# Moving side work in a two-layer encoder kernel: output-weight sums, token-tile loads, a b21 load and one product of the output pairs

## The chip, the cores and the metric

The kernel runs on one core of one Trainium2 chip. The time is the device time of one execution in microseconds; the figure for a kernel is the median over several executions. The engines are TensorE (PE in the profile, with its weight loads as PEld), VectorE (DVE), ScalarE (ACT), GpSimd (POOL) and SyncE (SP), which issues most of the transfers. Each engine runs its own instructions in order; semaphores order them between engines. The transfers go over 16 DMA engines.

## The reference

The input is 2048 prompt tokens and 512 sample tokens with 1024 channels, each going through two layers and a last norm.

```python
def attention_layer(x, g, w_in, w_out, sink, rel_bias):
    h = rmsnorm(x, g)
    z = h @ w_in                      # q (1024), k (256), v (256), gate (1024)
    o = banded_gqa_with_sink(q, k, v, rel_bias, sink)   # 16 heads, 4 kv heads, |i - j| <= 128
    return x + (o * jax.nn.silu(gate)) @ w_out

def fourier_layer(x, g, w_gate, w_out):
    h = rmsnorm(x, g)
    f = jnp.fft.fftn(h.reshape(b, s, 4, 256), axes=(1, 3), norm="ortho").real.reshape(b, s, d)
    gate = h @ w_gate
    return x + (f * jax.nn.silu(gate)) @ w_out

# trunk: attention_layer, fourier_layer, rmsnorm(x, final_norm)
```

`rmsnorm` divides each token's row by the root of its mean square, so it needs the sum of squares of every row of x.

## The kernel before

All arithmetic is in fp32. A product of two fp32 matrices is made from parts: each operand is split into a high part and the rest, and `matmul3` (L92) issues three matmuls, hi x hi, hi x lo and lo x hi. Splits are made by a cast on ScalarE (the high part) and a subtraction on VectorE or GpSimd (the low part).

**The attention phase** (L134) works through five chunks of 512 tokens: chunk 0 is the sample, chunks 1 to 4 the prompt. For each chunk, `make_h` (L170) loads the transposed tokens (xk), `kv_proj` (L267) makes keys and values, and then a loop of 69 steps i runs over eight head pairs p of eight steps each (four blocks of 128 queries, two heads). In step i stand: the scores of one block and head (TensorE spt, L422), bias and minimum (VectorE S, L434), the exp (ScalarE S, L438), reciprocal and scaling (VectorE, L441 and L444); three steps later the transposes of that block (TensorE pt, L461), which wait for the scaled exps, with their split (ScalarE L462, VectorE L463); two steps after that the product with the values (av, L475) and, every second block, that is every four steps, `out_evac` (L480): VectorE's sums o (L492), GpSimd's o times the gate s (L494), ScalarE's cast uT (L495) and GpSimd's lower part uT (L496). In between are the projections of the next head pair (`qg_proj`), as filling for TensorE, and in the last head pair the output projection `out_proj` (op, L94 to L96).

Into the same loop go side jobs, at steps that are written out by hand:

- `stats(c + 1)` (L143), for the next chunk: for each of its four or five token tiles (the prompt's first three chunks read one tile past their end) one step loads the tile (SP, xs, L151, 512 KB) and squares it with a sum (ScalarE, L152); a last step makes the inverse root (`inv_rms`, VectorE L88 and GpSimd L89). The steps lie at i = 28, 32, 36 and so on. At i = 56 `spread` (L157) transposes the result (TensorE L166) and copies it (ScalarE L167).
- `EXTRA[c]` (L629), for chunks 1 to 4: `gate_sums` (load, lower, sums, more) and `out_sums` (load, two sums, four splits) prepare sums of quarters of the gate weight and of the output weight of the Fourier layer, for products in Strassen's manner (seven products in place of eight). Each makes a quarter of the work per chunk. The loads are w32g (L575) and w32e (L607), the sums run in pieces of 256 columns on GpSimd (L565), the splits cast on ScalarE (L581 wB21, L622 eT1, eT3, eT2, eN4), and GpSimd issues the stores to b21d, sumd and the four ftd arrays.
- `AHEAD` in chunk 4 loads what the Fourier phase reads first.

The tiles xs, w32g, w32e, wB21, the four e tiles and (from chunk 1 on) xk share one ring of four buffers (`xtile`, L80): a load or a cast into the next buffer waits until what was in it four tiles ago is read, or has been stored. In chunk 0 the raw rows of the output weight (w32o, L111) use the same ring. Where an instruction is put into the order by hand, `after` (L129) ties it behind the last exp issued.

**The Fourier phase** (L744) makes the gates of the second layer pair by pair (`Pair`, `gates`, L881): W, Z and X are accumulators, the hooks between the products prepare the next pair. The product X (`x_step`, L888) uses four b21 tiles per pair, which `more()` (L873) loads on SP into a ring of 16 buffers; each `x_step` calls `more()` once after its matmuls, as long as tiles are left, and two are loaded ahead at the start. For the last pair the hooks load the rows of the output weight (w32f, `f_load`), the gathered gates (s2) and the first position transforms, whose results us are transposed by `split_T` (tru, L777).

Behind it come the position transforms and the output product. For the last groups (position pairs k1 = 1, 7, 3, 5 of the prompt) class `Outs` (L1138) makes the output product of two tiles of 128 tokens in Strassen's manner. `operands` (L1178) transposes the two tiles, makes the four sums F and splits them into S[1] to S[4], and splits the tiles' own quarters into A (`own`). `products` (L1191) adds the products into the rows xa and xb: W = A[0,0]*wo[0:4], Z = S1*T1, then T2 (in `third`), S4 with wo[12:16], S3*T3, X = A[0,1]*wo[4:8] and A[1,1]*N4. hooks[2] holds the operands of the next pair (`turns`, with its transposes, and the loads that go with it). X completes xa, which is then normed (`normed`: ScalarE's Square jkf, `inv_rms`, VectorE's scaling L1117, and the store). N4 completes xb. In the last pair xb is squared and written in halves.

Of the kernel before, what the change touches and what calls it, by code (L numbers as in the profile page):

```python
# [8 lines left out]
F32 = mybir.dt.float32  # L9
# [3 lines left out]
AF = mybir.ActivationFunctionType  # L13
# [5 lines left out]
P = 128  # L19
D = 1024  # L20
# [24 lines left out]
def encoder(  # L45
# [34 lines left out]
    def xtile(shape, dtype, name):  # L80
        return xp.tile(shape, dtype, align_bytes=LINE, tag="x", bufs=4, name=name)
# [4 lines left out]
    def inv_rms(ss, n, name):  # L86
        inv = main.tile([P, 8], F32, tag="inv", bufs=2, name=name)
        DVE.tensor_scalar(inv[:, :n], ss[:, :n], 1.0 / D, EPS, ALU.mult, ALU.add)  # L88
        POOL.tensor_tensor(inv[:, :n], inv[:, :n], mhalf[:, :n], ALU.pow)  # L89
        return inv  # L90
# [38 lines left out]
    def after(ins, anchor):  # L129

        if anchor is not None:
            tc.add_manual_dep(ins.ins, anchor.ins.name, ISSUE, reason="issue order")

    def attention_phase():  # L134

        with ExitStack() as es:
# [6 lines left out]
            def stats(c):  # L143

                tok, lo_t, hi_t = CHUNKS[c]
                nt = min(640, hi_t - tok) // P
                ss = main.tile([P, 8], F32, tag="ss", bufs=2, name=f"ss{c}")

                def one(i):
                    xt = xtile([P, D], F32, f"xs{c}_{i}")  # L150
                    after(SP.dma_start(xt, x[tok + i * P : tok + (i + 1) * P, :]), last_exp[0])  # L151
                    sq = ACT.activation(xt, xt, AF.Square, accum_out=ss[:, i : i + 1])  # L152
                    after(sq, last_exp[0])

                return [lambda i=i: one(i) for i in range(nt)] + [lambda: inv_rms(ss, nt, f"inv{c}")]

            def spread(c, inv, place=None):  # L157

# [467 lines left out]
                where = (("T1", 0, 1), ("T3", 1, 1), ("T2", 0, 0), ("N4", 1, 0))  # L626
                return [load, lambda: sums(0), lambda: sums(1)] + [lambda a=a: split(*a) for a in where]

            EXTRA = {c: dict(zip((4, 8, 12, 16, 18, 20, 22, 25, 30, 34, 38), gate_sums(c - 1) + out_sums(c - 1))) for c in range(1, 5)}  # L629

            def quarters(place, k):

# [111 lines left out]
    def fourier_phase(tail):  # L744
        with ExitStack() as es:
# [119 lines left out]
            def prod(out, a, b, ks, first):  # L865

                for k in ks:
                    cs = slice(k * P, (k + 1) * P)
                    matmul3(out, (a[0][:, cs], a[1][:, cs]), b[k], first and k == 0, k == 3, not first)
# [3 lines left out]
            def more():  # L873

                k = len(b21)
                if k < 4 * len(pairs):
                    t = right([P, 2, 512], F32R, f"b21_{k}")
                    SP.dma_start(f32(t), f32(b21d[k % 4]))
                    b21.append((t[:, 0], t[:, 1]))

            def gates(pr, hooks):  # L881

                n, A, S = pr.n, pr.A, pr.S
                W = psum2.tile([P, 512], F32, tag="acc", name=f"W{n}")
                Z = psum2.tile([P, 512], F32, tag="acc", name=f"Z{n}")
                X = bank(f"X{n}")

                def x_step(k):  # L888
                    prod(X, A[0, 1], b21[4 * n : 4 * n + 4], (k,), True)
                    more()  # L890

                def silu(c, i, half):
                    th = main.tile([P, 512], F32, tag="xr", bufs=3, name=f"gt{pr.ts[i]}_{half}")
                    ACT.activation(th, c, AF.Tanh, scale=0.5)
                    DVE.scalar_tensor_tensor(th, th, 1.0, c, ALU.add, ALU.mult)
                    t = pr.ts[i]
                    dst, t0 = (s2d[0], t) if t < SEQ // P else (s2d[1], t - SEQ // P)
                    POOL.dma_start(dst[t0 * P : (t0 + 1) * P, half * 512 : half * 512 + 512], th)

                def hook(i):  # L900
                    for h in hooks.get(i, ()):
                        h()

                four = range(4)
                c = xtile([P, 2, 512], F32, f"c{n}")
                c11, c22 = c[:, 0], c[:, 1]
                prod(W, A[0, 0], wg["B11"], four, True)
                ACT.copy(c11, W)
                hook(0)
                x_step(0)  # L910
                prod(Z, S[1], wg["T1"], four, True)
                ACT.copy(c22, Z)
                hook(1)
                prod(W, S[2], wg["T2"], four, False)
                c12 = fp.tile([P, 512], F32, tag="c12", bufs=1, name=f"c12_{n}")
                ACT.copy(c12, W)
                hook(2)
                x_step(1)
                prod(Z, S[4], wg["B22"], four, False)
                DVE.tensor_tensor(c12, c12, Z, ALU.add)  # L920
                silu(c12, 0, 1)
                hook(3)
                x_step(2)
                prod(W, S[3], wg["T3"], four, False)
                DVE.tensor_tensor(c22, c22, W, ALU.add)
                silu(c22, 1, 1)
                hook(4)
                x_step(3)
                DVE.tensor_tensor(c11, c11, X, ALU.add)
                silu(c11, 0, 0)  # L930
                hook(5)
                prod(W, A[1, 1], wg["N4"], four, False)
                silu(W, 1, 0)
                hook(6)
# [81 lines left out]
            pr = pairs[0]  # L1016
# [97 lines left out]
            def normed(x2, r):  # L1114

                inv = sumsq(x2, f"f{r[0]}")
                DVE.scalar_tensor_tensor(x2, x2, inv[:, 0:1], gfb, ALU.mult, ALU.mult)  # L1117
                SP.dma_start(out_rows(r), x2)
# [19 lines left out]
            class Outs:  # L1138
# [39 lines left out]
                def operands(self):  # L1178
                    self.turn(0, 0)
                    self.own(0, 0)  # L1180
                    self.turn(1, 0)
                    self.turn(1, 1)
                    self.sums(1)
                    self.sums(2)
                    self.turn(0, 1)
                    self.sums(4)
                    self.sums(3)
                    self.own(0, 1)
                    self.own(1, 1)

                def products(self, hooks, last=False):  # L1191
                    A, S, four = self.A, self.S, range(4)
                    (xa, xb), q = self.x2, (slice(0, 512), slice(512, 1024))
                    W = psum2.tile([P, 512], F32, tag="acc", name=f"Wo{self.n}")
                    Z = psum2.tile([P, 512], F32, tag="acc", name=f"Zo{self.n}")

                    def add(t, half, ps):
                        DVE.tensor_tensor(t[:, q[half]], t[:, q[half]], ps, ALU.add)

                    prod(W, A[0, 0], wo[0:4], four, True)  # L1200
                    add(xa, 0, W)
                    hooks[0]()
                    prod(Z, S[1], ft["T1"], four, True)
                    add(xb, 1, Z)

                    def third():
                        prod(W, S[2], ft["T2"], four, False)
                        add(xa, 1, W)

                    hooks[1](third)  # L1210
                    prod(Z, S[4], wo[12:16], four, False)
                    add(xa, 1, Z)
                    prod(W, S[3], ft["T3"], four, False)
                    add(xb, 1, W)
                    hooks[2]()
                    X = bank(f"Xo{self.n}")
                    prod(X, A[0, 1], wo[4:8], four, True)
                    add(xa, 0, X)
                    normed(xa, self.us[0][1])
                    if last:  # L1220
                        ss = main.tile([P, 8], F32, tag="ss", bufs=2, name="ssl")
                        junk = fp.tile([P, 512], F32, tag="c12", bufs=1, name="jkl").bitcast(BF16)
                        ACT.activation(junk[:, :512], xb[:, q[1]], AF.Square, accum_out=ss[:, 1:2])
                    prod(W, A[1, 1], ft["N4"], four, False)
                    add(xb, 0, W)
                    if not last:
                        normed(xb, self.us[1][1])
                        return
                    ACT.activation(junk[:, :512], xb[:, q[0]], AF.Square, accum_out=ss[:, 0:1])
                    DVE.tensor_tensor(ss[:, 0:1], ss[:, 0:1], ss[:, 1:2], ALU.add)  # L1230
                    inv = inv_rms(ss, 1, "invl")
                    for half in range(2):
                        hs = q[half]
                        DVE.scalar_tensor_tensor(xb[:, hs], xb[:, hs], inv[:, 0:1], gfb[:, hs], ALU.mult, ALU.mult)
                        (SP, ACT)[half].dma_start(out_rows(self.us[1][1])[:, hs], xb[:, hs])
# [292 lines left out]
```

## Time and profile before

| | |
|---|---|
| median of 3 runs | 1666.85 us (1666.19 to 1668.32) |
| the profiled execution: its own time | 1663.9 us |
| its span, first to last instruction | 1662.1 us |
| granted TensorE clock, mean | 0.996 |
| TensorE busy | 1630.8 us, 98% of the span |
| VectorE busy | 1200.5 us, 72% |
| ScalarE busy | 892.8 us, 54% |
| GpSimd busy | 444.9 us, 27% |
| moved by DMA | 367.75 MB, mean 221 GB/s |

A row of the profile gives the engine, the line of the code, the operation, the tile that is written and the tiles that are read. In brackets stands how long the engine was idle ahead of it and what ended that. Rows of waits have the total in us, how many times, and the longest. Attention takes the span up to about 1100 us, the Fourier phase the rest.

### The profile page before, as it was taken

To read this page: it belongs to the slowest core of one execution; us is meant where nothing else is said; L and a number is where in the kernel's file an instruction comes from. 1 tells how busy PE (TensorE), PEld (TensorE's weight loads), DVE (VectorE), ACT (ScalarE), POOL (GpSimd) and SP (SyncE) were. 2 spreads that over 40 slices of the span, in tenths; PEclk is the share of its full clock that TensorE was granted. 3 is DMA by queue.
4 is the path that set the end of the run, shared out by engine and by line. 5 is a ranking of instruction groups with operands and counts; after the bars stand their busy time and mean duration, and the time that the engine had idled before them with its cause. 6 is when DMAs were issued, how large, how long until landed. Compare 5 with 4: busy or idle time off the path is not lost.

```text
span 1662.1 us, 25836 instructions
## 1 busy us (share of the span) xinstructions
PE 1630.8 (98%) x8939; PEld 1401.0 (84%) x8939; DVE 1200.5 (72%) x2851; ACT 892.8 (54%) x2035; POOL 444.9 (27%) x623
## 2 busy tenths in 40 slices
PE   9999999999999999999999999999999999999997
PEld 7888788888898888988888888888888887888885
DVE  6787666878548786478783588858667667888685
ACT  6788634666236664256661466646555455343342
POOL 2456642322404222223214232221112121101010
PEclk9999999999999999999999999999999999999998
DMA  7486886564865555754548745656566468455952
GB/s 300 155 301 242 295 324 223 186 234 141 292 228 187 196 190 195 268 218 171 222 144 318 253 173 197 222 187 254 188 216 234 171 218 333 169 190 196 357 181 79
DMA packets 98909, 367.75 MB, mean 221 GB/s; under 512 B 11947, under 2 KB 22187, under 8 KB 81372
## 3 DMA queue, kind: packets, MB, share of 16 engines
q1 hardware_dynamic: 75948, 276.93, 47.7%
q0 software_dynamic: 21360, 88.13, 13.5%
q8 instruction: 71, 1.16, 0.3%
q10 hardware_dynamic: 1472, 1.05, 0.2%
q14 instruction: 58, 0.48, 0.1%
HBM read 279.01 MB, written 87.06 MB: 220 GB/s over the span
## 4 chain that ended last, share of the span: by engine, by line
PE 70%; DVE 9%; ACT 7%; DMA 6%; issue 5%; POOL 2%; SPq 0%; POOLq 0%; DVEq 0%; ACTq 0%
PE av L475 5%; PE spt L422 5%; PE pt L461 4%; PE op L94 4%; PE op L96 4%; PE op L95 4%; PE qp L94 3%; PE gp L94 3%; PE gp L96 3%; PE qp L96 3%; PE gp L95 3%; PE qp L95 3%; DMA xs<-in_x_dram 2%; ACT S L438 2%; PE W L95 2%
## 5 line engine op out<-in xcount | busy, mean ns | idle before, releaser
L438 ACT ACTIVATE S<-S 128x385 f32<-128x385 f32 (+1 forms) x320 | 191.0, 597 | 66.0 <-DVE S L434 64.3
L463 DVE TENSOR_TENSOR pts<-pt,pts 128x384 fp32r<-128x384 f32 (+1 forms) x320 | 168.3, 527 | 43.4 <-ACT pts L462 40.9
L462 ACT CAST pts<-pt 128x384 fp32r<-128x384 f32 (+1 forms) x320 | 143.4, 452 | 87.4 <-PE pt L461 83.4
L434 DVE CUSTOM_DVE_ANT_0 S<-spt,b 128x385 f32<-128x385 f32 (+1 forms) x320 | 168.5, 527 | 30.0 <-PE spt L422 27.1
L422 PE MATMUL spt<-kwin,qab 128*128 128x384 f32 (+1 forms) x640 | 157.7, 328 | 1.0 <-DVE S L434 1.0
L461 PE MATMUL pt<-ident,S 128*128 128x128 f32 x896 | 150.7, 273 | 6.2 <-ACT S L438 3.4
L494 POOL TENSOR_TENSOR o<-o,s 128x256 f32<-128x256 f32 x75 | 55.4, 738 | 341.3 <-DVE o L492 335.8
L422 PEld LDWEIGHTS spt<-kwin,qab 128*128 128x128 f32 x640 | 117.8, 188 | 28.2 <-DVE S L434 3.6
L475 PEld LDWEIGHTS av<-pts,v 128*128 128x128 f32 x896 | 126.3, 189 | 15.9 <-DVE pts L463 3.3
L475 PE MATMUL av<-pts,v 128*128 128x256 f32 x896 | 137.3, 286 | 2.1 <-DVE qab L371 1.1
L94 PE MATMUL gp<-h,wg 128*128 128x512 f32 x320 | 137.8, 431 | 0.0
L94 PE MATMUL qp<-h,wq 128*128 128x512 f32 x320 | 137.0, 428 | 0.3 <-DVE v L336 0.3
L461 PEld LDWEIGHTS pt<-ident,S 128*128 128x128 f32 x896 | 113.4, 140 | 21.7 <-ACT S L438 4.0
L94 PE MATMUL op<-wo,uT 128*128 128x512 f32 x320 | 126.5, 397 | 1.6 <-ACT invb L167 0.8
L96 PE MATMUL qp<-h,wq 128*128 128x512 f32 x320 | 126.0, 394 | 0.0
L96 PE MATMUL gp<-h,wg 128*128 128x512 f32 x320 | 125.9, 393 | 0.0
L95 PE MATMUL qp<-h,wq 128*128 128x512 f32 x320 | 125.8, 393 | 0.0
L95 PE MATMUL op<-wo,uT 128*128 128x512 f32 x320 | 125.8, 393 | 0.0
L95 PE MATMUL gp<-h,wg 128*128 128x512 f32 x320 | 125.8, 393 | 0.0
L96 PE MATMUL op<-wo,uT 128*128 128x512 f32 x320 | 124.8, 391 | 0.0
L444 DVE TENSOR_SCALAR S<-S 128x384 f32<-128x384 f32 (+1 forms) x256 | 115.9, 453 | 8.0
L441 DVE RECIPROCAL S<-S 128x1 f32<-128x1 f32 x320 | 51.3, 161 | 73.9 <-ACT S L438 70.7
(415 smaller groups left out, 4266.2 us busy)
## 6 DMA issues: line engine op xcount, KB each, us to landing
wo<-wsd SPq DMA_DIRECT2D x32, 1024.0 KB, 5.1
wq<-wsd SPq DMA_DIRECT2D x31, 1024.0 KB, 4.8
wg<-wsd SPq DMA_DIRECT2D x31, 1024.0 KB, 5.9
x<-x1d SPq DMA_DIRECT2D x40, 512.0 KB, 3.8
b<-b21d SPq DMA_DIRECT2D x40, 512.0 KB, 5.6
b<-rowd SPq DMA_DIRECT2D x40, 384.0 KB, 4.5
xs<-in_x_dram SPq DMA_DIRECT2D x23, 512.0 KB, 6.1
s2d<-gt POOLq DMA_DIRECT2D x40, 256.0 KB, 3.7
```

Source lines behind the costliest of these rows:

```text
L94: PE.matmul(out, a[0], b[0], start=start, stop=False, skip_group_check=more)
L95: PE.matmul(out, a[0], b[1], start=False, stop=False, skip_group_check=more)
L96: PE.matmul(out, a[1], b[0], start=False, stop=stop, skip_group_check=more)
L422: PE.matmul(ps[:, 2 + k0 * P : 2 + k1 * P], q, kwin[g][:, part, b * P + k0 * P : b * P + k1 * P], start=part == 0, stop=part == 1,)
L434: DVE.tensor_tensor_reduce(out=s[:, e0:e1], in0=ps[:, 1 + e0 : 1 + e1], in1=st["bias"][:, j, 386 - e1 : 386 - e0][:, ::-1], scale=1.0, sca ...
L438: last_exp[0] = ACT.activation(s[:, e0:e1], s[:, e0:e1], AF.Exp, bias=mn, scale=-1.0, accum_out=den)
L444: DVE.tensor_scalar(s[:, ks], s[:, ks], den, None, ALU.mult)
L461: PE.transpose(ps[:, kb, :], s[:, 1 + kb * P : 1 + (kb + 1) * P], ident)
L462: ACT.copy(hi[:, k0:k1, j, :], ps[:, k0:k1, :])
L463: DVE.tensor_tensor(lo[:, k0:k1, j, :], ps[:, k0:k1, :], f32(hi[:, k0:k1, j, :]), ALU.subtract)
L475: PE.matmul(out, v, pt[:, kb].rearrange("p h q -> p (h q)"), start=kb == k0 and part == 0, stop=kb == k1 - 1 and part == 1,)
L494: eng.tensor_tensor(o, o, s, ALU.mult)
```

## The change

Four edits, none of which changes what is computed:

1. In `stats`, the step that loads tile i no longer squares it; it squares tile i - 1. There is one step more, so each Square and the inverse root come one step of this list, four steps of the loop, later.
2. The steps of `EXTRA` move from 4, 8, 12, 16 (gate weight) and 18, 20, 22, 25, 30, 34, 38 (output weight) to 2, 4, 6, 8 and 10, 12, 14, 16, 18, 20, 22.
3. In the last pair of gates, `more()` is called once more after the first step of X, so that the last b21 tile's load is issued there and not a step later.
4. In `Outs`, the product X with its sum, and xa's norm, are moved: X goes ahead of hooks[2], the norm behind hooks[2], and T3 with its sum behind both. In `operands`, the split of A[0,1] goes ahead of the third sum.

```diff
@@ -146,13 +146,18 @@
                 nt = min(640, hi_t - tok) // P
                 ss = main.tile([P, 8], F32, tag="ss", bufs=2, name=f"ss{c}")
 
+                xs = []
+
                 def one(i):
-                    xt = xtile([P, D], F32, f"xs{c}_{i}")
-                    after(SP.dma_start(xt, x[tok + i * P : tok + (i + 1) * P, :]), last_exp[0])
-                    sq = ACT.activation(xt, xt, AF.Square, accum_out=ss[:, i : i + 1])
-                    after(sq, last_exp[0])
-
-                return [lambda i=i: one(i) for i in range(nt)] + [lambda: inv_rms(ss, nt, f"inv{c}")]
+
+                    if i:
+                        sq = ACT.activation(xs[i - 1], xs[i - 1], AF.Square, accum_out=ss[:, i - 1 : i])
+                        after(sq, last_exp[0])
+                    if i < nt:
+                        xs.append(xtile([P, D], F32, f"xs{c}_{i}"))
+                        after(SP.dma_start(xs[i], x[tok + i * P : tok + (i + 1) * P, :]), last_exp[0])
+
+                return [lambda i=i: one(i) for i in range(nt + 1)] + [lambda: inv_rms(ss, nt, f"inv{c}")]
 
             def spread(c, inv, place=None):
 
@@ -626,7 +631,7 @@
                 where = (("T1", 0, 1), ("T3", 1, 1), ("T2", 0, 0), ("N4", 1, 0))
                 return [load, lambda: sums(0), lambda: sums(1)] + [lambda a=a: split(*a) for a in where]
 
-            EXTRA = {c: dict(zip((4, 8, 12, 16, 18, 20, 22, 25, 30, 34, 38), gate_sums(c - 1) + out_sums(c - 1))) for c in range(1, 5)}
+            EXTRA = {c: dict(zip((2, 4, 6, 8, 10, 12, 14, 16, 18, 20, 22), gate_sums(c - 1) + out_sums(c - 1))) for c in range(1, 5)}
 
             def quarters(place, k):
 
@@ -908,6 +913,9 @@
                 ACT.copy(c11, W)
                 hook(0)
                 x_step(0)
+                if pr is pairs[-1]:
+
+                    more()
                 prod(Z, S[1], wg["T1"], four, True)
                 ACT.copy(c22, Z)
                 hook(1)
@@ -1184,8 +1192,8 @@
                     self.sums(2)
                     self.turn(0, 1)
                     self.sums(4)
+                    self.own(0, 1)
                     self.sums(3)
-                    self.own(0, 1)
                     self.own(1, 1)
 
                 def products(self, hooks, last=False):
@@ -1210,13 +1218,13 @@
                     hooks[1](third)
                     prod(Z, S[4], wo[12:16], four, False)
                     add(xa, 1, Z)
-                    prod(W, S[3], ft["T3"], four, False)
-                    add(xb, 1, W)
-                    hooks[2]()
                     X = bank(f"Xo{self.n}")
                     prod(X, A[0, 1], wo[4:8], four, True)
                     add(xa, 0, X)
+                    hooks[2]()
                     normed(xa, self.us[0][1])
+                    prod(W, S[3], ft["T3"], four, False)
+                    add(xb, 1, W)
                     if last:
                         ss = main.tile([P, 8], F32, tag="ss", bufs=2, name="ssl")
                         junk = fp.tile([P, 512], F32, tag="c12", bufs=1, name="jkl").bitcast(BF16)
```

In the instructions of the changed program each load of a token tile is at least four steps ahead of its Square. On SP the w32e loads stand right behind the weights wg of head pair 3 and ahead of wq of head pair 4, where they stood behind these; the last b21 load stands six loads further ahead. On GpSimd the sequence in a chunk is: sums of w32g, wB21's lower part, the store to b21d, the stores to sumd, the first o and uT of the chunk, the eight pieces of the w32e sums, the next o and uT; before, three pairs of o and uT stood ahead of the w32e sums.

## The prediction

> **What bounds the kernel now.** The first thing read is the head of the page.
>
> ```profile
> span 1662.1 us, 25836 instructions
> PE 1630.8 (98%) x8939; PEld 1401.0 (84%) x8939; DVE 1200.5 (72%) x2851; ACT 892.8 (54%) x2035; POOL 444.9 (27%) x623
> ```
>
> TensorE is busy for 1630.8 of 1662.1 us. No product is added or taken away by this change, so at most the 31.3 us that TensorE stands still can be won, and everything below is about which of those it removes and which it makes. The view of waits by engine, restricted to TensorE, tells what they are; it names only those that the semaphores show.
>
> ```profile
> engine line waited for: us in total, times, longest us
> PE pt L461 <- ACT S L438: 3.4, 2, 2.2
> PE pt L461 <- DVE S L444: 2.5, 2, 1.3
> PE X L94 <- DMA b<-b21d: 2.0, 1, 2.0
> ...
> PE Ap L95 <- DVE gp L1070: 0.7, 3, 0.3
> ```
>
> The largest two are transposes of the attention (pt) that wait for a softmax: ScalarE's exp was late. Next comes one product X that waits for a load of b21. So the question is what makes ScalarE late. The waits of all engines have the line:
>
> ```profile
> ACT xs L152 <- DMA xs<-in_x_dram: 22.8, 9, 4.7
> ```
>
> Nine times ScalarE stood at the Square of a token tile until that tile's load had landed, up to 4.7 us. ScalarE runs in order, so the exps behind stood too. Whether TensorE paid for it shows in its busy time around these Squares (20 us windows: TensorE, its weight loads, VectorE, ScalarE, GpSimd; then the granted clock, the DMA share, GB/s):
>
> ```profile
> 140.00:160.00 20.00, 18.77 (x107) 15.95 (x107) 14.79 (x52) 17.88 (x42) 11.97 (x17) 1.00 0.74 282
> 160.00:180.00 20.00, 17.88 (x103) 14.71 (x102) 16.08 (x58) 16.61 (x44) 16.03 (x24) 1.00 0.95 358
> 340.00:360.00 20.00, 19.60 (x111) 16.36 (x109) 14.97 (x44) 13.49 (x35) 6.86 (x10) 1.00 0.62 211
> 360.00:380.00 20.00, 18.74 (x106) 15.88 (x107) 15.73 (x52) 13.63 (x35) 4.19 (x6) 1.00 0.76 270
> 560.00:580.00 20.00, 18.79 (x108) 16.10 (x107) 14.01 (x42) 12.39 (x30) 5.16 (x8) 1.00 0.70 229
> 580.00:600.00 20.00, 17.63 (x100) 14.74 (x99) 14.56 (x45) 12.33 (x33) 4.94 (x7) 1.00 0.69 249
> 800.00:820.00 20.00, 19.89 (x112) 16.61 (x110) 15.29 (x47) 13.36 (x34) 6.56 (x10) 1.00 0.60 223
> 820.00:840.00 20.00, 18.92 (x110) 16.55 (x111) 17.88 (x55) 13.43 (x36) 3.57 (x5) 1.00 0.43 160
> 1040.00:1060.00 20.00, 20.00 (x118) 17.57 (x117) 16.72 (x56) 13.46 (x36) 4.57 (x7) 1.00 0.53 184
> ```
>
> TensorE stood still for 1.66 us in chunk 1 (40 less 19.60 and 18.74), 3.58 in chunk 2 and 1.19 in chunk 3: together 6.43 us. In the last chunk, which has no token tiles to square, the same place is full (20.00 of 20). In chunk 0 3.35 us are lost, but there ScalarE itself is at 17.88 of 20, so not all of that is a wait.
>
> **Token loads a step ahead.** One of the Squares, the 10 us around it, the landing of all 23 tile loads, and a product o of GpSimd (one comes every four steps):
>
> ```profile
> 795.69 1.06 ACT L152 ACTIVATE xs<-xs 128x1024 f32<-128x1024 f32 x1 [2.92 <-DMA xs<-in_x_dram]
> 790.00:800.00 10.00, 10.00 (x61) 8.76 (x60) 6.37 (x21) 6.72 (x18) 2.62 (x4) 1.00 0.82 296
> DMA to landing us min/median/max: 3.2/6.1/10.1
> 518.00 0.74 POOL L494 TENSOR_TENSOR o<-o,s 128x256 f32<-128x256 f32 x1 [7.46 <-DVE o L492]
> 527.01 0.74 POOL L494 TENSOR_TENSOR o<-o,s 128x256 f32<-128x256 f32 x1 [7.01 <-DVE o L492]
> ```
>
> The tile loads land after 6.1 us, 10.1 at most. Load and Square are issued in the same step now. In the changed program a load stands four steps ahead of its Square, which is 9.0 us (518.00 to 527.01). It can also start earlier, since the output weight's sums, which use the same four buffers, end at step 22 and not at 38. So nearly every load has the time that it needs, and the waits end: **-6.4 us** in chunks 1 to 3, and nothing if the loads still come late (0 to -6.4). The 2.92 us wait at 795.69 is worth a look: TensorE was full around it (10.00 of 10). So ScalarE can be up to 2.9 us late before TensorE stops; as the exps are not everywhere as far ahead, I use 2.4 as this slack below.
>
> In chunk 0 the Squares move four steps later, into the stretch at 17.88 of 20, and the loads of the output weight wait for the buffers that they free. A Square of 1.06 us arriving in a full stretch costs up to +1.2 with its read of the sum; against it stands up to 2.4 us of waiting at Squares that goes (22.8 us in all, of which chunk 0 has little). I take about a third of the 3.35 us, **-1.2**, range -2.4 to +1.2.
>
> **The sums move up.** They are the same instructions on GpSimd, two to sixteen steps earlier. What moves is what stands behind them: GpSimd's product o and its split uT of the attention output, on which ScalarE's cast waits. Chunk 1 and chunk 2 of before (the o at 518.00 is above):
>
> ```profile
> 275.71 1.64 POOL L565 TENSOR_TENSOR w32g<-w32g,w32g 128x256 f32<-128x256 f32 x2 [29.73 <-DMA w32g<-in_w_gate_dram]
> ...
> 296.36 0.74 POOL L494 TENSOR_TENSOR o<-o,s 128x256 f32<-128x256 f32 x1 [7.00 <-DVE o L492]
> 495.89 1.43 POOL L565 TENSOR_TENSOR w32g<-w32g,w32g 128x256 f32<-128x256 f32 x2 [40.67 <-DMA w32g<-in_w_gate_dram]
> ...
> 532.07 1.44 POOL L565 TENSOR_TENSOR w32e<-w32e,w32e 128x256 f32<-128x256 f32 x2 [3.07 <-DMA w32e<-in_w_fout_dram]
> DMA to landing us min/median/max: 3.0/5.3/13.5
> DMA to landing us min/median/max: 6.3/7.0/7.4
> ```
>
> The last two lines are the landings of b21d's transfers and of the w32e loads. In the changed order the eight w32e pieces stand on GpSimd ahead of the o that was at 518.00; before, they came at 532.07, after it. Their second load takes a buffer that comes free only when b21d's store has landed. So in chunk 2: start 495.89, eight pieces of 0.72 and one store of about 0.6 make 6.4, landing of the store 5.3, of the load 7.0, then eight pieces 5.9 (532.07 to 537.9, where o followed): 520.5, and o is 2.5 us late. Chunk 1 by the same sum from 275.71: 300.3 against 296.36, 3.9 late. Chunks 3 and 4 have the same distances as chunk 2 to within half a microsecond; I take 2.5 for each. Less the slack of 2.4: 1.5 in chunk 1 and 0.1 in each other one, **+1.8**. The range is 0 (landings of 3.0 and 6.3 take 3.0 off, and only chunk 1 would be late, by less than the slack) to +5.8 (each a microsecond later). Before, the o's own operands came last ([7.46 <-DVE o]), so these sums would be the new thing that ScalarE waits for, through "uT <- POOL o". The splits behind (T1 to N4) are one cast of 0.6 us each on ScalarE, two steps apart (4.5 us); the windows above have ScalarE under 70% busy in chunks 1 to 3, and I cost them nothing. If a buffer's store is late there, the cast waits and it costs what the Squares cost now.
>
> **The last b21 load.** The chain ahead of the product X:
>
> ```profile
> 1373.24 0.56 SPq L878 DMA_DIRECT2D b<-b21d  x1
> 1384.61 2.35 DVE L1107 TENSOR_TENSOR us<-us,s2s 128x1024 f32<-128x1024 f32 x2
> 1386.78 0.50 PE L94 MATMUL X<-b,tTb 128*128 128x512 f32 x1 [2.00 <-DMA b<-b21d]
> 1387.58 1.69 PE L777 MATMUL tru<-ident,us 128*128 128x128 f32 x14
> 1403.91 0.80 PE L94 MATMUL fo<-wo,tTu 128*128 128x512 f32 x1 [1.25 <-ACT wo L1285]
> ```
>
> The extra call puts this load ahead of six others on SP's queue; six issues of 0.56 put it at about 1369.9. Even with the longest landing of b21d's loads above, 13.5 us, it is there at 1383.4, before TensorE comes to X at 1384.78 (1386.78 less 2.00). X takes 0.8 and ends at 1385.6, but the transposes behind it need us, whose two products end at 1385.8 and 1386.96: 0.2 to 1.4 of the 2.0 us, I take 0.7, stay as a wait for VectorE. **-1.3**, range -2.0 to 0. The six loads that it passes come some 1.3 us later; the next stall, at 1403.91, is ScalarE's split of wo, which hangs on casts that follow TensorE's own pace, so I let it shift along unchanged.
>
> ```profile
> 1400.00:1405.00 5.00, 3.56 (x17) 2.29 (x16) 4.73 (x11) 4.16 (x12) 0.00 (x0) 0.85 1.03 418
> 1405.00:1410.00 5.00, 5.00 (x27) 4.35 (x26) 4.62 (x8) 3.86 (x8) 0.54 (x1) 0.81 1.03 415
> ```
>
> Around this next stall the granted clock falls to 0.85 and 0.81; without it 0.15 and 0.19 of 5 us, 1.7 us, would come back. I leave it in place and let -1.7 widen the low end. [...]
>
> **The product X of the Outs pairs.** It is now issued ahead of the next pair's turns and of T3, in three pairs and in the end. In the inner pairs its split of A[0,1] moves ahead of the third sum; the price is bounded by the largest wait of this stretch on each side, 0.7 us of TensorE in all (Ap above) and this one:
>
> ```profile
> 1574.57 1.23 DVE L1107 TENSOR_TENSOR up<-up,s2p 128x1024 f32<-128x1024 f32 x1 [2.22 <-DMA s2p<-s2d,mir]
> ```
>
> There the gather of s2p waits for a buffer until xb's output is written; xb's end moves back by VectorE's row-norm work, some 0.8 us, xa's forward. TensorE was not waiting there, so I take **+0.3**, range -0.5 to +2.2.
>
> **The tail.** Behind the last product:
>
> ```profile
> 1647.95 0.69 DVE L1198 TENSOR_TENSOR x<-x,Xo 128x512 f32<-128x512 f32 x1 [2.03 <-PE Xo L96]
> 1650.24 0.39 PE L96 MATMUL Wo<-fN,tT 128*128 128x512 f32 x1
> 1650.79 1.28 DVE L1117 SCALAR_TENSOR_TENSOR x<-x,invf,gfb 128x1024 f32<-128x1024 f32 x1 [0.73 <-POOL invf L89]
> 1651.99 0.68 DVE L1198 TENSOR_TENSOR x<-x,Wo 128x512 f32<-128x512 f32 x1
> ```
>
> TensorE's last sum is there at about 1650.65 (1650.24 and 0.39), but VectorE is at the other row's norm (1650.79, 1.28 us) and adds it at 1651.99. With X one product of twelve matmuls earlier (2.72 us) that norm runs from 1648.07 to 1649.35, T3's add from there to 1650.04, and the last add starts at 1650.65: 1.3 earlier, and all behind it moves along. **-1.3**, range -1.4 to -0.7 (if the add of T3 comes in between later).
>
> **Sum**: -6.4 -1.2 +1.8 -1.3 +0.3 -1.3 = -8.1 us. The profiled run took 1663.9 us (1.8 around its span of 1662.1); it becomes 1655.8. It lies 2.95 below the median of the runs shown, 1666.85, so the forecast for the median is **1658.7 us**.
>
> **Rivals.**
> - The loads are still late. The first token tiles take the buffers of the sums' splits, which come free when their stores have landed; if these are slow, the step ahead is lost and the waits of 6.4 us and chunk 0's 1.2 stay, while b21 and the tail give 2.6 and GpSimd takes 1.8: 1666.85 -2.6 +0.3 +1.8 = 1666.4, no change. Against it: the sums end six steps before the first tile load.
> - The reordered Outs pairs cost: X waits for its split, or the gather's 2.22 us reaches TensorE in each of the three pairs, +6.7 in place of +0.3: 1658.7 +6.4 = 1665.1, within the noise. Against it: TensorE's waits there are 0.3 us now.
> - Slower: the sums hold GpSimd. One mechanism, in all four chunks: with L the landing of the second w32e load, TensorE loses 1.8 + 4 x (L - 7.0). All other terms make -9.9, so it is level at L = 9.0 and slower by 0.2% from L = 9.9; at the 10.1 that a tile load has shown it costs 14.2 and the time is 1666.85 -9.9 +14.2 = 1671. For it: the chunk's DMA share is 0.6 to 0.8 and the load now runs beside the sums' three stores. Against it: the eight w32e loads lie between 6.3 and 7.4. [...]
> - More: chunk 0 gives 2.4, GpSimd costs nothing, the clock's 1.7 comes back and the rest as forecast: -6.4 -2.4 -2.0 -0.5 -1.4 -1.7 = -14.4, 1652.5.
>
> **Chances.** Forecast 0.68, loads still late 0.12, Outs pairs 0.05, slower 0.12, more 0.03. A change of under 0.2%, 3.3 us, can't be told from none here. Faster by more than that: 0.68 and 0.03, with a little of the forecast falling short, 0.71; same 0.17; slower 0.12. The range: from the best case, 1652.5, up to 1667, which takes in the two cases without change and leaves out the slower one.
>
> **What would show it.** Right: no Square at L152 waits for its load in chunks 1 to 3, and TensorE is at 20.00 in 340 to 380, 560 to 600 and 800 to 840 or where these steps then lie; X <- b21d is gone from TensorE's waits; the last add on VectorE starts with TensorE's last sum. The w32e pieces would show "<- DMA w32e" right after the sumd stores, and ScalarE's uT <- POOL o a wait of 2 to 5 us once a chunk. Wrong: these waits above 5 us in every chunk with TensorE's idle time beside them (slower), Squares that still wait (no change), or a new wait of the product Xo or of the gather in the pairs 7, 3 and 5.

## The result and the profile after

| | before | changed |
|---|---|---|
| median | 1666.78 us (1665.89 to 1670.75, 6 runs) | 1661.26 us (1660.06 to 1662.93, 6 runs) |
| profiled execution, its span | 1663.9, 1662.1 us | 1662.93, 1661.1 us |

The ratio is 0.9963 with a 95% interval of 0.995 to 0.9976; by the medians the change is 5.5 us faster. A second set of executions of the same changed kernel beside its own runs of before (1662.68 us in 11 runs, 1665.11 in 15) gave 0.9983 (0.9974 to 0.9992), 2.4 us by the medians. Forecast were 8.1 us. The two profiled executions lie only 1.0 us apart, since that of before lies 2.9 us below its median and that of the change 1.7 above its own; so the traces are compared stretch by stretch.

The rows of TensorE's waits in the changed kernel, which stand against those of before:

```profile
PE pt L466 <- DVE S L449: 4.1, 4, 2.1
PE Wo L94 <- DVE x L1206: 2.2, 1, 2.2
PE op L94 <- ACT invb L172: 1.6, 1, 1.6
PE pt L466 <- ACT S L452: 1.4, 2, 0.7
PE fo L94 <- ACT wo L1293: 1.3, 1, 1.3
...
PE tru L782 <- DVE us L1115: 0.7, 2, 0.5
```

X no longer waits for b21; tru waits for us in its place. The transposes pt still wait for a softmax, only elsewhere, op waits 1.6 us for invb, the copied inverse root (0.8 before), and there is a new wait that the prediction did not have: Wo, which is N4, for VectorE's x, 2.2 us. The view of all waits names the softmax's new reason; first a row of before, then rows of the changed kernel:

```profile
ACT uT L495 <- POOL o L494: 63.6, 58, 2.1
```

```profile
ACT uT L500 <- POOL o L499: 100.5, 67, 5.2
...
POOL w32e L570 <- DMA w32e<-in_w_fout_dram: 21.9, 4, 5.9
...
POOL eT L570 <- ACT eT L627: 19.7, 12, 3.3
```

ScalarE's longest wait at uT rose from 2.1 to 5.2 us, GpSimd waits 21.9 us for the w32e loads (11.0 before), and the Squares' line is nearly empty. In the tile view of xs, the 22.8 us have become this:

```profile
  DMA xs<-in_x_dram: 0.3, 1
```

The windows where the Squares had stopped TensorE (the changed kernel, columns as before):

```profile
340.00:360.00 20.00, 20.00 (x118) 17.53 (x117) 16.56 (x53) 14.95 (x40) 3.46 (x5) 1.00 0.48 178
360.00:380.00 20.00, 20.00 (x117) 17.49 (x116) 16.99 (x58) 14.34 (x37) 2.94 (x4) 1.00 0.65 228
560.00:580.00 20.00, 20.00 (x116) 17.45 (x115) 17.03 (x52) 13.93 (x35) 3.33 (x5) 1.00 0.50 178
580.00:600.00 20.00, 20.00 (x119) 17.60 (x118) 17.35 (x55) 14.81 (x37) 3.55 (x6) 1.00 0.61 225
800.00:820.00 20.00, 20.00 (x118) 17.55 (x117) 17.45 (x55) 15.17 (x39) 3.98 (x5) 1.00 0.58 203
820.00:840.00 20.00, 20.00 (x117) 17.50 (x116) 17.55 (x52) 13.43 (x34) 2.94 (x4) 1.00 0.45 151
```

They are full: this part of the change did what it should. What was given back stands in two places. The first is the eight pieces, the sums of w32e in steps of 256 columns on GpSimd. In chunk 1, GpSimd's timeline of the changed kernel:

```profile
281.55 0.57 POOL L588 DMA_DIRECT2D b21d<-wB  x1
...
295.91 1.55 POOL L570 TENSOR_TENSOR w32e<-w32e,w32e 128x256 f32<-128x256 f32 x2 [5.53 <-DMA w32e<-in_w_fout_dram]
297.42 1.43 POOL L570 TENSOR_TENSOR w32e<-w32e 128x256 f32<-128x256 f32 x2
298.81 2.81 POOL L570 TENSOR_TENSOR w32e<-w32e,w32e 128x256 f32<-128x256 f32 x4
301.58 0.73 POOL L499 TENSOR_TENSOR o<-o,s 128x256 f32<-128x256 f32 x1
```

o was at 296.36 before and is at 301.58, behind the pieces. ScalarE stands for it, then TensorE, in the timelines of these engines:

```profile
302.34 0.40 ACT L500 CAST uT<-o 128x256 fp32r<-128x256 f32 x1 [4.99 <-POOL o L499]
```

```profile
304.16 0.52 PE L466 MATMUL pt<-ident,S 128*128 128x128 f32 x3 [2.13 <-DVE S L449]
```

The windows around it show a second price, the granted clock (third column from the end) in the 5 us behind the wait:

```profile
300.00:305.00 5.00, 2.87 (x18) 2.35 (x17) 1.54 (x6) 2.35 (x7) 3.03 (x5) 1.00 0.00 0
305.00:310.00 5.00, 5.00 (x22) 4.46 (x21) 4.70 (x17) 3.64 (x9) 2.24 (x4) 0.66 0.64 190
310.00:315.00 5.00, 5.00 (x30) 4.35 (x29) 3.49 (x13) 3.45 (x10) 3.29 (x5) 1.00 0.50 209
```

At 0.66, 22 matmuls are issued in these 5 us; in the same window of last_pair_old, behind a wait of 2.11, they are 32 at 1.00 (its rows stand in the last section). By an estimate from this row, 0.66 of 5 us being 3.3, 1.7 us are lost at the lower clock besides the 2.13 of the wait. The other place is the tail; first the last product's start in TensorE's timeline, then VectorE:

```profile
1643.80 0.39 PE L96 MATMUL Wo<-fT,S 128*128 128x512 f32 x1
1646.37 0.47 PE L94 MATMUL Wo<-fN,tT 128*128 128x512 f32 x1 [2.18 <-DVE x L1206]
```

```profile
1644.34 1.28 DVE L1125 SCALAR_TENSOR_TENSOR x<-x,invf,gfb 128x1024 f32<-128x1024 f32 x1 [0.73 <-POOL invf L89]
1645.55 0.68 DVE L1206 TENSOR_TENSOR x<-x,Wo 128x512 f32<-128x512 f32 x1
1650.98 0.69 DVE L1206 TENSOR_TENSOR x<-x,Wo 128x512 f32<-128x512 f32 x1 [4.75 <-PE Wo L96]
```

N4 adds into the accumulator W that T3 has just filled, so it may not begin until VectorE has read T3's sum out of it. VectorE reads it at 1645.55, behind xa's scaling. The clock fell here too, in the 5 us in which the wait ends:

```profile
1645.00:1650.00 5.00, 3.63 (x9) 2.87 (x10) 1.23 (x2) 0.72 (x2) 0.00 (x0) 0.67 0.26 105
```

Both kernels issue the same 8939 matmuls. The time from the start of one matmul to the start of another with the same number in a kernel's sequence can thus be subtracted between traces, clock and waits included. A table of such differences to the profiled run of before, in us (plus is slower), with kernels of the experiments that are told below:

| stretch (its place in before) | changed | changed again | loads and sums | b21 alone | loads ahead alone | sums behind o |
|---|---|---|---|---|---|---|
| chunk 0 loop, 86 to 211 | +0.6 | +0.6 | +0.7 | +0.9 | +0.7 | +0.7 |
| chunk 1, pieces of w32e, 280 to 332 | +3.9 | +3.8 | +4.1 | 0 | 0 | 0 |
| chunk 1, Squares, 332 to 413 | -2.9 | -2.9 | -2.9 | +0.3 | -2.9 | -2.9 |
| chunk 2, pieces, 495 to 538 | +0.6 | +0.8 | +0.8 | 0 | 0 | 0 |
| chunk 2, Squares, 538 to 630 | -4.6 | -4.6 | -4.6 | -1.4 | -4.6 | -4.6 |
| chunk 3, pieces | +0.4 | +0.6 | +0.2 | 0 | 0 | 0 |
| chunk 3, Squares | -1.9 | -1.9 | -1.9 | +0.1 | -1.6 | -2.0 |
| chunk 4, pieces | +1.8 | +1.9 | +2.0 | 0 | 0 | 0 |
| last gates, b21, 1377 to 1440 | -1.0 | -1.4 | -0.1 | -2.0 | -0.7 | -1.9 |
| inner Outs pairs, 1561 to 1616 | +0.2 | -0.7 | +0.6 | -0.4 | +0.2 | +0.1 |
| last pair to the last matmul | +4.2 | +4.1 | 0 | 0 | 0 | +2.6 |

"b21 alone" leaves the attention as it was, so its column shows by how much a stretch differs between two executions of the same code: up to 1.4 us at the Squares and 0.9 in chunk 0, but 0 at the pieces.

### The profile page after: what moved, and what is told of

Read it like the earlier page. It is cut to its first block, busy times and chain, and to the rows that moved or that the text cites. A ratio compares the mean times of both kernels' runs of the same rounds, so it can differ in the third digit from the quotient of the medians.

```text
span 1661.1 us, 25834 instructions
## 1 busy us (share of the span) xinstructions
PE 1632.6 (98%) x8939; PEld 1404.2 (85%) x8939; DVE 1201.1 (72%) x2851; ACT 890.5 (54%) x2035; POOL 441.7 (27%) x623
## 3 DMA queue, kind: packets, MB, share of 16 engines
q10 hardware_dynamic: 1472, 1.05, 0.2%
```

## The experiments

Each ran beside its own executions of the kernel before on one chip; the ratio is to those.

**sums_behind_o.** The pieces are tied behind GpSimd's uT, and the last six steps of the output weight's sums move to 13 to 24.

```diff
-zip((2, 4, 6, 8, 10, 12, 14, 16, 18, 20, 22), ...)
+zip((2, 4, 6, 8, 10, 13, 15, 18, 20, 22, 24), ...)
...
+                    else:
+                        last_lo[0] = lo
...
-                        pieces(b22, b22, b12, ALU.subtract)
+                        pieces(b22, b22, b12, ALU.subtract, last_lo[0])
...
```

> The changed kernel, with GpSimd's eight pieces of the output weight's sums tied behind uT of the block before (and the steps 13 to 24 in place of 12 to 22). Theory: in the changed kernel the pieces hold GpSimd's o until the w32e load has landed, which stops TensorE 2.30, 0.61, 0.43 and 1.43 us in chunks 1 to 4 and lowers its clock in chunk 1; behind o they stop nobody: 4.8 to 6.3 us below the changed kernel's 1661.3, so 1655 to 1656.5, no ScalarE wait of over 2 us at uT, and the Squares still wait for no load. Rival: the wait goes elsewhere (to the next o, to the splits' buffers, or back to the token tiles, which now get their buffers later): 1659 to 1662.

Measured: 1655.28 us against 1665.25, ratio 0.9941 (0.9925 to 0.9957). GpSimd's timeline in chunk 1 has o ahead of the pieces, and the window in which the changed kernel stood still is full:

```profile
297.84 0.73 POOL L499 TENSOR_TENSOR o<-o,s 128x256 f32<-128x256 f32 x1 [7.83 <-DVE o L497]
299.09 0.74 POOL L501 TENSOR_TENSOR uT<-o,uT 128x256 fp32r<-128x256 f32 x1 [0.52 <-ACT uT L500]
299.78 1.55 POOL L572 TENSOR_TENSOR w32e<-w32e,w32e 128x256 f32<-128x256 f32 x2
```

```profile
300.00:305.00 5.00, 5.00 (x33) 4.43 (x32) 4.90 (x14) 2.71 (x8) 5.00 (x7) 1.00 0.15 47
305.00:310.00 5.00, 5.00 (x31) 4.41 (x30) 4.02 (x14) 3.39 (x9) 2.80 (x5) 1.00 0.68 242
```

The clock stays at 1.00 too. All four stretches of the pieces fall to 0 in the table, and the Squares keep their gain: the pieces ahead of o were the cause, and in this trace the wait went nowhere else. In the two later kernels that hold this edit, both_mended and both_mended_t3, the pieces' stretch of chunk 1 kept 0.4 and 0.9 us.

**last_pair_old.** T3, X, N4 in the last pair as before; the inner pairs as changed.

```diff
+                    if last:
+                        lower()      # T3 and its sum
+                        cross()      # X and its sum
+                        normed(xa, self.us[0][1])
+                    else:
+                        cross()
+                        hooks[2]()
+                        normed(xa, self.us[0][1])
+                        lower()
```

> The changed kernel, with the last pair's products alone in the order of before (T3, X, N4). Theory: in the changed order N4 adds into the accumulator that T3 has just filled, so TensorE waits 2.2 us until VectorE, which does xa's norm first, has read T3's sum, and restarts at a lower clock (0.67 over 5 us, another 1.7); against it stands the 1.3 us that the last add gains. So 0.9 to 2.5 us faster than the changed kernel: 1658.8 to 1660.4. Rival: the prediction's own step, a gain of 1.3 from the new order: 1662.6.

Measured: 1658.77 us, ratio 0.9961 (0.9945 to 0.9976); from the same stretch of matmuls the last pair takes 0.2 us more than before, not 4.2, and the wait of Wo is gone from TensorE's. By the traces the direction is the theory's: the changed order costs the tail more than it brings. The times alone don't tell it, since the ratio's interval overlaps that of the change.

**last_pair_old_late_norm.** In addition xa's scaling is tied behind the last add:

```diff
-                        normed(xa, self.us[0][1])
+                        write = normed(xa, self.us[0][1], True)
...
-                    add(xb, 0, W)
+                    done = add(xb, 0, W)
+                    if last:
+                        write(done)
```

> As last_pair_old, and xa's scaling by its norm on VectorE is tied behind the last add of N4. Theory: TensorE doesn't wait, and the last add no longer waits 1.3 us for that scaling; the scaling now lies beside ScalarE's last Square and delays what follows by 0.4: 0.9 us faster than last_pair_old, so 1658 to 1659.5. Rival: the end is set by the stores, not by the last add: as last_pair_old.

Measured: 1659.79 us, 0.9969 (0.9957 to 0.9981), above the expected range by 0.3 us and not faster than last_pair_old in the times. In VectorE's timeline the last add does follow N4 at once, and the scaling comes behind it:

```profile
1647.62 0.69 DVE L1210 TENSOR_TENSOR x<-x,Wo 128x512 f32<-128x512 f32 x1 [0.61 <-PE Wo L96]
1648.22 1.28 DVE L1127 SCALAR_TENSOR_TENSOR x<-x,invf,gfb 128x1024 f32<-128x1024 f32 x1
```

From the last matmul's start to the last store's issue it is 4.74 us, in last_pair_old and before 5.79: the 1.05 are there, but smaller than what other places of the program spread by from one execution to the next: the pieces' stretch of chunk 1 alone took 4.3 us more than before in this trace and 2.5 in that of last_pair_old.

**outs_alone.** The kernel before with the Outs edits only (the diff's hunks at L1184 and L1210).

> The kernel before, with the edits in Outs alone (product X, xa's norm, T3, the split of A[0,1]). Theory: the tail loses 0.9 to 2.5 us as told for last_pair_old and the three inner pairs 0.5: 1668.2 to 1669.8 against 1666.8. Rival (the prediction): +0.3 in the pairs and -1.3 in the tail: 1665.8.

Measured: 1667.96 us against 1665.25, ratio 1.0014 (1.0002 to 1.0025). This edit alone makes the kernel slower, by 2.3 us after the ratio (0.3 to 4.2), just below the expected range. The last pair took 2.6 us more here, without a fall of the clock (1.00 from 1640 to 1655), and the end behind the last matmul 1.3 less.

**loads_and_sums.** The kernel before with the token loads and the steps of the sums (the hunks at L146 and L626).

> The kernel before, with the token loads a step ahead and the earlier steps of the sums, nothing else. Theory: the tile waits give 5.8 to 6.4 us, GpSimd's pieces take 4.8 and the clock in chunk 1 up to 1.5 more, chunk 0 takes 0.9: -0.1 to 0 by the profile that I have, but that profile was one of the slower executions; with the medians' 5.5 us less b21's 1.3 and plus the tail's 0.9 to 2.5 it is 1661 to 1664. Rival: nearly all of the measured gain is b21's and Outs': 1666.

Measured: 1661.9 us against 1666.39, 0.9975 (0.9964 to 0.9986). Within the theory's range, so the attention edits carry most of the gain. Its windows show the same fall of the clock as the changed kernel:

```profile
300.00:305.00 5.00, 2.65 (x17) 2.18 (x16) 1.49 (x7) 2.30 (x7) 3.39 (x5) 1.00 0.00 0
305.00:310.00 5.00, 5.00 (x22) 4.38 (x21) 4.73 (x16) 3.70 (x10) 2.02 (x3) 0.66 0.61 142
```

**b21_alone.** The kernel before with the extra `more()`.

> The kernel before, with the extra call of more() alone. Theory: TensorE's 2.0 us wait for b21 goes and 0.7 to 1.0 of it comes back as a wait for us: -1.0 to -1.3, 1665.5 to 1665.8. Rival: the loads that it passes come late and the next stall, fo at wo, grows: 1666.8 or more.

Measured: 1663.7 us against 1666.39, ratio 0.9992 (0.9982 to 1.0003): the median lies below the expected range, but by the ratio there is no difference that these runs can tell from none. TensorE's waits show the exchange that was forecast:

```profile
PE fo L94 <- ACT wo L1288: 1.3, 1, 1.3
...
PE tru L777 <- DVE us L1110: 1.0, 3, 0.5
```

The 2.0 us of X are gone, 1.0 is back at us, and the next stall, the product fo at ScalarE's split wo, stands at 1.3 as before, so the loads that were passed cost nothing there.

**chunk0_old_squares.** The changed kernel, with load and Square in one step for the tiles that are squared in chunk 0.

```diff
+                def one(i, lag=0 if c == 1 else 1):
...
+                    if i < nt and not lag:
+                        square(i)
```

> The changed kernel, but in chunk 0 (the squares of chunk 1's tiles) load and Square stay in one step. Theory: TensorE loses 12.4 us to its ideal pace in 120 to 180 in the changed kernel and 11.6 in the one before, so the later Squares cost up to 0.9 there: 1660.4 to 1661.3. Rival (the prediction): the later Squares gain 1.2: 1662.5.

Measured: 1661.99 us against 1666.39, 0.9982 (0.9973 to 0.9992), between the two ratios of the changed kernel and 0.7 us above the expected range. The chunk 0 stretch took 0.0 us more than before here, 0.6 in the changed kernel, but b21_alone and outs_alone, which have the same old Squares there, took 0.9 and 2.5 more. So the cost that the theory gave to the later Squares can't be told from the spread of single executions. The gain of 1.2 us that was forecast shows in no trace.

**both_mended.** sums_behind_o and last_pair_old_late_norm together.

> The changed kernel with sums_behind_o and last_pair_old_late_norm together. Theory: the two places are independent, so the gains add: 4.8 to 6.3 and 1.8 to 3.4 below 1661.3, 1651.6 to 1654.7. Rival: one of the places only moves its wait: 1655 to 1660.

Measured: 1653.68 us against 1666.39, ratio 0.993 (0.9917 to 0.9944), 7.6 us below the changed kernel's 1661.26 and within the expected range, as it should be if the gains of the two places add. The times don't show the second gain by itself: the interval overlaps that of sums_behind_o alone.

**changed_again.** The changed kernel once more, unedited.

> The changed kernel itself, beside the next three on one chip. Theory: the waits stand where they stood (N4 at T3's add 2.2 us, pt behind the w32e pieces in chunk 1 about 2.1), while the clock's fall behind them comes in some executions and not in others, so that single times spread by 2 to 3 us: median 1660 to 1662. Rival: the places themselves change from run to run.

Measured: 1662.68 us against 1665.11, 0.9983 (0.9974 to 0.9992), slightly above the range. The waits stand at the same places with the same length (Wo 2.2, pt up to 2.1), and the clock fell in chunk 1 again (0.70).

**t3_add_first.** xa's scaling in the last pair tied behind T3's add.

```diff
-                    normed(xa, self.us[0][1])
+                    write = normed(xa, self.us[0][1], last)
                     prod(W, S[3], ft["T3"], four, False)
-                    add(xb, 1, W)
+                    done = add(xb, 1, W)
+                    if last:
+                        write(done)
```

> The changed kernel, with xa's scaling in the last pair tied behind T3's add on VectorE. Theory: N4 waits for nothing but T3's add, which now starts with T3's sum: the wait falls from 2.2 to about 0.9 us (0.7 for the add, the rest for the semaphores), the scaling still ends ahead of N4's sum, and the last add starts with that sum: 1.3 us, or up to 3 with the clock, below the changed kernel. Rival: N4 waits for something else (the transposed tile, the weight): 2.2 us stay.

Measured: 1658.96 us, 0.9961 (0.9947 to 0.9975), against 1662.68 of changed_again beside it. TensorE's timeline:

```profile
1645.08 0.47 PE L94 MATMUL Wo<-fN,tT 128*128 128x512 f32 x1 [0.87 <-DVE x L1210]
```

The wait is 0.87 in place of 2.18 us, the stretch costs 1.3 in place of 4.1. So it is T3's add, held up by the scaling, that N4 waited for. With the 1.3 us that are gained behind the last matmul, this order is about level with that of before, and no better.

**loads_ahead_alone.** The kernel before with the hunk in `stats` alone.

> The kernel before, with load and Square a step apart and nothing else; the sums keep their late steps. Theory: one step of 9 us is enough for most loads, so that most of the 9.4 us (by stretches of equal instructions) go without the earlier sums, and the w32e pieces hold nobody: 1657.5 to 1660. Rival: the sums' splits hold the four buffers until step 38, the loads are issued no earlier and the waits at the Squares stay: 1664 to 1667.

Measured: 1655.53 us against 1665.11, ratio 0.9944 (0.993 to 0.9957); 2 us faster than the expected range's low end. Its windows:

```profile
300.00:320.00 20.00, 20.00 (x117) 17.51 (x116) 16.16 (x51) 12.62 (x32) 8.80 (x12) 1.00 0.52 178
360.00:380.00 20.00, 20.00 (x118) 17.53 (x117) 16.91 (x56) 15.27 (x41) 3.36 (x5) 1.00 0.74 260
580.00:600.00 20.00, 20.00 (x117) 17.50 (x116) 17.30 (x55) 15.04 (x38) 2.94 (x4) 1.00 0.71 254
```

One of the four edits gives all that the change gains and more: 9.6 us by the medians against 2.4 of the whole change beside it. All Squares together wait 0.3 us for their loads here, as in the changed kernel. So the buffers, which the sums still held until step 38, made no Square wait, and the earlier sums weren't needed for it.

**both_mended_t3.** sums_behind_o and t3_add_first together.

> The changed kernel with sums_behind_o and t3_add_first together. Theory: -6.7 us of the pt waits and -1.3 to -3 of the tail: 1652 to 1654.5, as both_mended or 0.3 better, since the end behind the last product is 1.3 shorter than in the kernel before and only 0.9 of wait is paid for it. Rival: the tail's wait brings the lower clock with it again and both_mended is 1 to 2 us faster.

Measured: 1654.21 us against 1665.11, 0.9933 (0.9919 to 0.9946), the same as both_mended by the intervals. Either is faster than both the kernel before and the changed one; loads_ahead_alone overlaps with them.

## Why the prediction was right, and where not

Faster was right, and 1661.26 lies in the range; of the 8.1 us forecast, 5.5 came, and 2.4 in the second set. That the total came out this near is in part luck: terms were off by several us in both directions, and the errors partly cancelled.

- **Token loads a step ahead** (-6.4): the mechanism held, the term was mis-sized. By equal matmuls the three stretches give -2.9, -4.6 and -1.9, together -9.4 us in the same trace, and the medians of loads_ahead_alone give 9.6. Against the two other traces that have the old Squares, b21_alone and outs_alone, it is 8.5 and 9.8. The step that failed is reading TensorE's standstill from busy time in windows: a matmul's busy time overlaps with its neighbour's, as in TensorE's timeline of before, with 0.40 us each at starts 0.23 apart,

```profile
174.93 0.40 PE L95 MATMUL op<-wo,uT 128*128 128x512 f32 x1
175.16 0.40 PE L96 MATMUL op<-wo,uT 128*128 128x512 f32 x1
```

  so a row at 17.63 of 20 has lost more than 2.37: it holds 100 matmuls, the full window of the changed kernel 119.
- **Chunk 0** (-1.2): nothing of it is seen (+0.6 in the table, within the spread). What TensorE gained there (av and spt wait 0.9 us less) it lost at other waits. In 86 to 212 it waits 1.4 us for pt <- ACT S and 1.6 for op <- ACT invb in the changed kernel, 0.3 and 0.8 in before; loads_ahead_alone has 1.4 and 1.7, and chunk0_old_squares 0.3 and 0.8 again. Before and changed, at the second of them:

```profile
174.59 0.51 PE L94 MATMUL op<-wo,uT 128*128 128x512 f32 x1 [0.84 <-ACT invb L167]
```

```profile
174.61 0.50 PE L94 MATMUL op<-wo,uT 128*128 128x512 f32 x1 [1.65 <-ACT invb L172]
```

  TensorE is there 0.8 us sooner and starts at the same time, since ScalarE, which works without a pause from 171.82 in the trace of before and from 172.15 in that of the change, makes its copy no sooner (173.97 and 173.99). Why pt waits longer stays open.
- **The sums move up** (+1.8): right in its mechanism and place, too small. GpSimd's o came 4.8 us late in chunk 1 (301.58 against 296.36, less the 0.4 by which the changed trace was behind there); in chunk 2, 3.5 (522.81 against 518.00, less 1.3). Forecast were 3.9 and 2.5. The waits of TensorE, without the clock, sum to about 5 us, near the +5.8 that the term's range gave for "each a microsecond later". The slack of 2.4 was about right, as 4.8 late cost 2.1 and 3.5 late cost 0.6. What failed is the landing of 7.0. The tile view of w32e in the changed kernel, that in loads_ahead_alone, where the sums keep their late steps, and that of wB in the changed kernel, the store to b21d:

```profile
DMA to landing us min/median/max: 8.8/9.5/10.2
DMA to landing us min/median/max: 6.5/7.1/7.7
DMA to landing us min/median/max: 2.9/2.9/3.1
```

  That is the mechanism of the slower rival, with L at 9.5; its price formula asked 11.8 us there, because it kept all else of the sum as it was. But the store landed in 2.9 us where the sum had 5.3, and in chunk 1 the load was issued 10.4 us after the start of the sums (286.15 less 275.77) and not 11.7, so that o came only about 1 us later than forecast. Another 1.7 us, by the estimate above, came with the lower clock (0.66), for which the sum had no term here. The rival's ground for a longer landing was that the load now runs beside the sums' three stores. The median landing is 8.9 to 9.7 us in all ten traces that issue the load early and 7.0 to 7.5 in the four that issue it late. That agrees with it, though it is not shown: no run separates the sums' own stores from the other transfers.
- **The last b21 load** (-1.3): right in its mechanism, and in size about 1 us. Traces are compared here in which the clock's fall at the next stall is present in both or absent in both. With the fall (the lowest window of 5 us there at 0.66 to 0.81), the two of the change have -1.0 and -1.4, and those without the extra call 0 (before), -0.1 (loads_and_sums) and -0.7 (loads_ahead_alone); without the fall (1.00 throughout), b21_alone has -2.0 and outs_alone -1.0. In times the term is too small to be told. The 1.7 us that the range's low end gave to this fall were an estimate from two rows; outs_alone, without the call and without the fall, lies 1.0 below before.
- **The Outs pairs** (+0.3): nothing in the inner pairs that stands out of -0.7 to +0.6.
- **The tail** (-1.3): wrong, by the step "T3's add from there to 1650.04, and the last add starts at 1650.65". It let N4 run through while T3's add waited. But X had been the cover between T3's sum and N4, in the same accumulator; moving X away uncovered a wait of 2.2 us. Behind the last matmul the 1.3 us were gained as worked out; so the tail lost 1.3 us (2.6 less 1.3), and 2.9 when the clock fell with it (4.2 less 1.3). With T3's add first (t3_add_first) the wait was 0.87. None of the rivals had this wait.

All terms, for the profiled run: -9.4 (Squares), +6.7 (pieces and clock), -1.0 (b21), +4.2 -1.3 (tail), and about -0.2 in the rest (chunk 0 +0.6, the start -0.2, the gates before the last pair -0.6, the inner pairs +0.2, rounding) make -1.0 between the spans, 1662.1 and 1661.1.

## What to carry to other kernels

An early load can be worth its whole wait while the work put in its neighbourhood eats it: when a block of side work moves on an engine, look for what stands behind it (GpSimd's o came 4.8 us late here), and don't price its load by the old landing (7.1 us issued late, 9.5 issued early). Before a product is moved, ask for which accumulator it was the cover (2.2 us of wait here). And try the parts alone: here one of the four edits, the load ahead of its Square, was worth more than all four.

## What the runs showed of the hardware

A wait of over 2 us on TensorE was followed by a lower granted clock in some executions and not in others of nearly the same code. Of seven traces with the wait behind the pieces in chunk 1, five have 0.66 to 0.70 over 305 to 310 (the changed kernel, changed_again, loads_and_sums, last_pair_old_late_norm, t3_add_first), and two have 1.00 (last_pair_old and chunk0_old_squares). Here is last_pair_old, whose wait was as long (2.11 us) as the changed kernel's (2.13):

```profile
300.00:305.00 5.00, 2.89 (x17) 2.32 (x16) 1.92 (x6) 2.35 (x7) 2.66 (x4) 1.00 0.00 0
305.00:310.00 5.00, 5.00 (x32) 4.42 (x32) 4.69 (x18) 3.64 (x9) 2.62 (x4) 1.00 0.68 220
```

The stretch cost +2.5 there and +3.9 in the changed kernel. So one wait had two prices here, 1.4 us apart; what decides between them, no run shows. That removing such waits narrows the spread of a kernel's times is not shown: the six runs of both_mended lie over 3.8 us, the six of the change over 2.9.
